# Moving the rows of the 64x64 inverses from GpSimd to VectorE in a DeltaNet decoder step, with their blocks packed in DRAM

## The chip, the cores and the metric

The kernel runs on one core of a Trainium2 chip. The core has a matrix engine (PE in the profile) with its weight load (PEld), VectorE (DVE), ScalarE (ACT), GpSimd (POOL) and SyncE (SP), on whose queue all DMAs of this kernel are issued. Each engine runs its own instructions strictly in the order of the program and waits for the others by semaphores. The metric is the device time of one execution in microseconds; the program is timed several times and the median is given. One execution was also taken by the hardware profiler, and all rows shown here come from it.

## What is computed

A prompt of 1040 tokens (16 learned ones and 1024 given ones) and 64 sample tokens go through two decoder layers. The change touches the first mixer, a gated DeltaNet with 8 heads, in which every chunk of 64 tokens of a head needs the inverse of a unit lower triangular 64x64 matrix:

```python
kk = jnp.einsum('bhnid,bhnjd->bhnij', k, k)
lower = jnp.where(strict, beta[..., :, None] * kk * decay, 0.0)
T = lax.linalg.triangular_solve(lower + eye, jnp.broadcast_to(eye, lower.shape),
                                left_side=True, lower=True, unit_diagonal=True)
U = jnp.einsum('bhnij,bhnje->bhnie', T, v * beta[..., None])
W = jnp.einsum('bhnij,bhnjd->bhnid', T, k * (beta * jnp.exp(G))[..., None])
```

Before it stand the projections of q, k, v and z (the gate), a short causal convolution and SiLU on q, k and v, SiLU alone on z, and a normalisation of k. Everything else (the recurrence, the output projection, two ConvFFNs and a pooling mixer) is the same in both kernels.

## The kernel before

The projection stage makes 33 tiles of 128 output channels in the order of the list `order`: a tile with the decay inputs (`ba`), then k, v and z tiles of the first heads, k3 to k7, q0 to q7, and then v and z in turn from v2, z2 to v7, z7. A tile is three chunks of 368 tokens, c0 to c2. For a chunk PE runs 24 matmuls into one of four PSUM banks (`a_chunk`, `a_half`, `mm3`: three products of high and low halves for each of 8 blocks of input channels). For q, k and v the chunk is convolved: one scaling on ACT and three multiply-adds on DVE (L384), in c2 three more for the sample tokens (L389), then SiLU on ACT (L257). A z chunk goes from PSUM through SiLU on ACT and needs nothing of DVE. A bank is free again when ACT and DVE have read it. The weights come in tiles of 128x512, which ACT and POOL split in two halves (L154, L155, `wlo`), two for each tile. A finished tile is written to DRAM (`spill`, L512).

For every k tile a job (`k_steps`) follows that lies between the chunks of the next tiles: it loads the decay row `Gb` and the beta row `Bb` by a broadcast (L483, L484), makes the decay matrices `E` on DVE (L489), normalises k, multiplies k by itself on PE, multiplies the products by `E` into `Q` (L503), sets the diagonal on POOL (L504) and writes the 128x1152 tile `Q` to DRAM as `Qd` (L508).

After the last head the inverses begin (`inverses`, `invert`). 128 blocks of 64x64 (8 heads, 16 chunks) lie one to a partition in `Qb`, read from `Qd` by 16 DMAs (L541), and a set of 40 blocks of 16x16 for the last tokens lies in `Qt`, read by 5 DMAs (L545). For every column j an outer product (L529) and a subtraction (L531) are run on the columns behind it. Rows 0 to 9 of the inverse are on POOL (`Xa`, `ta`), rows 10 to 63 on DVE (`Xb`, `tb`), and the 16x16 blocks (`Xt`) use `tb` too. `tb` is also the source of a DMA that fills a DRAM tile with zeros (L553). The results are written to DRAM (`xb`), turned block by block (3 copies on DVE, one on POOL, L565 and L568), and written again (`xt`).

The inverses are a generator that the projection loop advances: after every chunk it gets `INV` more of a budget, and each step takes the cost that it yields. So the place of the inverse's instructions in DVE's and POOL's order is set when the program is built, by these numbers, and not by what has arrived. When it is done, the loads of head 0 and the first Newton step (`after_inverses`, `newton`) are put between the chunks that are left, and the recurrence over heads begins after the last tile, z7.

Of the kernel before, what the change touches and what calls it, by code (L numbers as in the profile page):

```python
# [10 lines left out]
F32 = mybir.dt.float32  # L11
F32R = mybir.dt.float32r
AF = mybir.ActivationFunctionType
ALU = mybir.AluOpType
# [3 lines left out]
P = 128  # L18
# [14 lines left out]
H = 8  # L33
# [5 lines left out]
GROUPS = ((0, 3), (3, 3), (6, 3))  # L39
NEWTON = ((0, 3), (3, 3), (6, 2))  # L40
GW = 384
PROWS = 10
TAIL0 = 1024
INV = 2.4
NTAIL = N_META + NSA


# [150 lines left out]
def build(nc, tc, I, O, stop=None):  # L198
    es = ExitStack()
    V, A, G, T, SY = nc.vector, nc.scalar, nc.gpsimd, nc.tensor, nc.sync  # L200
    slots = Slots()

    def pool(name, bufs=1, ctx=es, space=None, side=None):
        kw = {"reuse_waits": "tile", "side": side}
        if space == DRAM:
            kw = {"space": space}
        elif space == PSUM:
            kw = {"space": space, "reuse_waits": "tile"}
        return ctx.enter_context(tc.tile_pool(name=name, bufs=bufs, **kw))
# [124 lines left out]
    zd_d = [dr.tile([P, NTP], F32, name=f"zd{h}") for h in range(H)]  # L334
    Qd_d = dr.tile([H, P, NTP], F32, name="Qd")

    xb_d = dr.tile([P, 4096], F32, name="xb")
    xt_d = dr.tile([P, 4096], F32, name="xt")
    x8_d = dr.tile([H, NTAIL, NTAIL], F32, name="x8")
# [12 lines left out]

    AHEAD = 4
    order = [("ba", 0), ("k", 0), ("k", 1), ("k", 2), ("v", 0), ("z", 0), ("v", 1), ("z", 1)]
    order += [("k", h) for h in range(3, H)] + [("q", h) for h in range(H)]
    for h in range(2, H):
        order += [("v", h), ("z", h)]
    base = {"q": 0, "k": 8, "v": 16, "z": 24}
    tid = [32 if kd == "ba" else base[kd] + h for kd, h in order]

# [41 lines left out]
    def l2norm(dst):  # L402

        while busy:
            yield 1
        busy.append(dst)
        sq = ab.tile([P, NT], F32, tag="sq", name="sq")
        rr = ab.tile([P, NT], F32, tag="rr", name="rr")
        A.activation(sq, dst[:, :NT], AF.Square)
        yield 3  # L410
        hl = []
        for c in range(NCH):
            hl.append([kp.tile([P, CH], F32R, tag=nm, name=nm, bufs=3) for nm in ("sqh", "sql")])
# [12 lines left out]
        busy.pop()
# [51 lines left out]
    def k_steps(h, kT):  # L478
        while busy or not rows[0].done or h > 1 and not kj[h - 2].done:
            yield 1  # L480
        Gb = kp.tile([P, NTP], F32, tag="Gb", name="Gb")
        Bb = kp.tile([P, NTP], F32, tag="Bb", name="Bb")
        SY.dma_start(out=Gb, in_=grow_d[h:h + 1, :].partition_broadcast(P))  # L483
        SY.dma_start(out=Bb, in_=brow_d[h:h + 1, :].partition_broadcast(P))  # L484
        E = kp.tile([P, NTP], F32, tag="E", name="E", bufs=2)
        for u in range(NU):
            s = slice(u * P, (u + 1) * P)
            m = cm[:, K_MF:K_MF + P] if u < 8 else cm[:, K_MT:K_MT + P]
            V.scalar_tensor_tensor(E[:, s], Gb[:, s], cols[:, u, 1, h:h + 1], m,  # L489
                                   op0=ALU.subtract, op1=ALU.add)  # L490
        yield from l2norm(kT)
        A.activation(E, E, AF.Exp)
        G.tensor_tensor(E, E, Bb, op=ALU.mult)
        Q = kp.tile([P, NU, P], F32, tag="Q", name="Q", bufs=2)
        yield 7
        SY.dma_start(out=kd_d[h], in_=kT)
        for g0, gn in GROUPS:
            ps = px.tile([P, 3, P], F32, tag="px", name="kk")
            for u in range(gn):
                s = slice((g0 + u) * P, (g0 + u + 1) * P)  # L500
                T.matmul(ps[:, u, :], kT[:, s], kT[:, s], start=True, stop=True)
            q = Q[:, g0:g0 + gn, :]
            V.tensor_tensor(q, ps, v3(E[:, g0 * P:(g0 + gn) * P]), op=ALU.mult)  # L503
            G.affine_select(q, q, pattern=[[0, gn], [1, P]], compare_op=ALU.not_equal, fill=1.0,  # L504
                            base=0, channel_multiplier=-1)
            yield 1
        yield 1
        SY.dma_start(out=Qd_d[h], in_=flat(Q))  # L508

    def spill(dd, t):  # L510
        yield 2
        SY.dma_start(out=dd, in_=t)  # L512

    def invert(parts, Qb, n, m):


        for eng, r0, X, tmp in parts:
            G.memset(X[:n], 0.0)
            G.memset(X[:n].rearrange("p a b -> p (a b)")[:, r0::m + 1], 1.0)
        yield 1.0  # L520
        for j in range(m - 1):
            w = m - 1 - j
            cost = 0.0
            for eng, r0, X, tmp in parts:
                k = min(j + 1 - r0, X.shape[1])
                if k <= 0:
                    continue
                t = tmp[:n, 0:k * w].rearrange("p (a b) -> p a b", b=w)
                eng.tensor_tensor(t, X[:n, 0:k, j:j + 1].to_broadcast([n, k, w]),  # L529
                                  Qb[:n, j:j + 1, j + 1:m].to_broadcast([n, k, w]), op=ALU.mult)  # L530
                eng.tensor_tensor(X[:n, 0:k, j + 1:m], X[:n, 0:k, j + 1:m], t, op=ALU.subtract)  # L531
                cost = max(cost, 0.25 + k * w * (0.0033 if eng is G else 0.0021))
            yield cost

    def inverses(sp):
        Qb = sp.tile([P, 64, 64], F32, name="Qb")
        Qt = sp.tile([P, 16, 16], F32, name="Qt")
        for h in range(H):
            for a in range(2):
                src = Qd_d[h][64 * a:64 * a + 64, :].rearrange("j (u t) -> u j t", t=P)  # L540
                SY.dma_start(out=Qb[64 * a + 8 * h:64 * a + 8 * h + 8], in_=src[0:8, :, 64 * a:64 * a + 64])  # L541
        nt = NTAIL // 16
        for a in range(nt):
            r = slice(16 * a, 16 * a + 16)
            SY.dma_start(out=Qt[8 * a:8 * a + 8], in_=Qd_d[:, r, TAIL0 + 16 * a:TAIL0 + 16 * a + 16])  # L545
        Xa = sp.tile([P, PROWS, 64], F32, name="Xa")
        Xb = sp.tile([P, 64 - PROWS, 64], F32, name="Xb")
        ta = sp.tile([P, PROWS * (64 - PROWS)], F32, name="ta")
        tb = sp.tile([P, 1024], F32, name="tb")
        t8 = tb[:NTAIL, :H * NTAIL]  # L550
        Xt = sp.tile([P, 16, 16], F32, name="Xt")
        G.memset(t8, 0.0)
        SY.dma_start(out=x8_d.rearrange("h p t -> p h t"), in_=v3(t8, NTAIL))  # L553
        yield 6.0
        tail = invert([(V, 0, Xt, tb)], Qt, 8 * nt, 16)
        for cost in invert([(G, 0, Xa, ta), (V, PROWS, Xb, tb)], Qb, P, 64):
            next(tail, None)
            yield cost
        for a in range(nt):
            r = slice(16 * a, 16 * a + 16)  # L560
            SY.dma_start(out=x8_d[:, r, 16 * a:16 * a + 16], in_=Xt[8 * a:8 * a + 8])
        XT = Qb.rearrange("p b a -> p a b")
        SY.dma_start(out=xb_d[:, 0:64 * PROWS], in_=flat(Xa))
        SY.dma_start(out=xb_d[:, 64 * PROWS:], in_=flat(Xb))
        G.tensor_copy(XT[:, 0:PROWS, :], Xa)  # L565
        for r in range(0, 64 - PROWS, 18):
            n = min(r + 18, 64 - PROWS)
            V.tensor_copy(XT[:, PROWS + r:PROWS + n, :], Xb[:, r:n, :])  # L568
            yield 1.0
        SY.dma_start(out=xt_d, in_=flat(Qb))  # L570
        yield 1.0
# [72 lines left out]
    with ExitStack() as en:  # L644
# [16 lines left out]
        for nm in ("sq", "rr"):  # L661
            t = ab.tile([P, NT], F32, tag=nm, name=nm)
# [450 lines left out]
    r0 = []  # L1113
# [418 lines left out]
    for pos, (l, i, hf, c) in enumerate(units):  # L1532
# [23 lines left out]
        n = 0  # L1556
# [138 lines left out]
```

## Time and profile before

| | us |
|---|---|
| median of 3 runs | 2599.67 |
| lowest and highest | 2596.69 and 2604.51 |
| time of the profiled execution | 2598.88 |
| span of its trace | 2597.1 |
| PE busy | 2410.2 (93%) |
| DVE busy | 1647.3 (63%) |
| POOL busy | 1167.5 (45%) |
| ACT busy | 1022.4 (39%) |

The profiled execution's own time is 1.8 us more than its span; the span is what the trace covers. The share of an engine is over the whole span and mixes stages with different limits. The stage of this change ends 541 us after the start of the span.

### The profile page before, as it was taken

The page shows a single profiled execution, that of the slowest core. Times are in us where ns is not written, and L with a number is a line of the kernel's source. Part 1 is how long each engine was busy: PE and PEld are TensorE (multiplying, and loading weights), DVE is VectorE, ACT ScalarE, POOL GpSimd, SP SyncE. Part 2 cuts the span into 40 slices and gives each one's busy share as a digit, 9 for nine tenths or more (in the row PEclk, how much of TensorE's full clock was granted, in tenths as well). Part 3 has the DMA queues.
Part 4 walks back from the last instruction along what each step waited for, and adds up shares of the span by engine and source line. Part 5 has one row for each costly group of instructions (what it writes and reads, how often), then busy time and mean ns, then how long its engine had stood idle before and what let it go on. Part 6 is the DMA issues. An engine that isn't in the chain of part 4 may idle for free.

```text
span 2597.1 us, 38494 instructions
## 1 busy us (share of the span) xinstructions
PE 2410.2 (93%) x14341; PEld 2350.7 (91%) x14341; DVE 1647.3 (63%) x3139; ACT 1022.4 (39%) x2165; POOL 1167.5 (45%) x1232
## 2 busy tenths in 40 slices
PE   6899588978999889999999999888999999999997
PEld 5898587978888789999999999877899999999996
DVE  7678399856666655555555546887964555555556
ACT  5667122255454543222222344445354323222234
POOL 3456388644554443233322455466465333233342
PEclk9999799999999999999999999999999999999999
DMA  3254612467552211111111133233433111111112
GB/s 132 96 178 170 97 70 78 143 215 237 173 167 67 75 57 50 41 49 41 49 41 41 62 106 106 82 104 110 91 102 107 50 49 41 41 49 45 46 53 81
DMA packets 139802, 233.31 MB, mean 90 GB/s; under 512 B 48848, under 2 KB 59472, under 8 KB 139360
## 3 DMA queue, kind: packets, MB, share of 16 engines
q1 hardware_dynamic: 139616, 230.86, 27.4%
q8 instruction: 113, 1.85, 0.3%
q14 instruction: 73, 0.60, 0.1%
HBM read 191.77 MB, written 39.04 MB: 89 GB/s over the span
## 4 chain that ended last, share of the span: by engine, by line
PE 67%; DVE 18%; issue 4%; ACT 4%; POOL 3%; DMA 2%; SPq 2%; DVEq 0%; POOLq 0%; ACTq 0%
PE up L265 12%; PE up L263 12%; PE up L264 12%; PE dn L265 6%; PE dn L263 6%; PE dn L264 6%; DVE acc L384 2%; POOL wlo L155 2%; DVE tb L529 2%; PE ps L263 2%; DVE Xb L531 2%; PE ps L264 2%; PE ps L265 2%; DVE nhf L318 1%; SPq L541 1%
## 5 line engine op out<-in xcount | busy, mean ns | idle before, releaser
L155 POOL TENSOR_TENSOR wlo<-wst,whi 128x512 fp32r<-128x512 f32 x470 | 629.2, 1357 | 515.1 <-ACT whi L154 503.9
L263 PE MATMUL up<-hhi,whi 128*128 128x370 f32 (+2 forms) x2112 | 708.9, 336 | 0.7 <-ACT hhi L321 0.7
L264 PE MATMUL up<-hlo,whi 128*128 128x370 f32 (+2 forms) x2112 | 699.8, 331 | 2.7 <-DVE hlo L324 1.8
L265 PE MATMUL up<-hhi,wlo 128*128 128x370 f32 (+2 forms) x2112 | 701.6, 332 | 0.0
L1272 DVE SCALAR_TENSOR_TENSOR acc<-up,cv,acc 128x368 f32<-128x368 f32 (+4 forms) x528 | 303.7, 575 | 625.1 <-ACT acc L1264 387.6
L1336 DVE TENSOR_TENSOR xT<-xT,dn 128x368 f32<-128x368 f32 (+1 forms) x864 | 409.0, 527 | 2.3 <-PE dn L265 2.3
L264 PEld LDWEIGHTS up<-hlo,whi 128*128 128x128 f32 x2112 | 401.8, 190 | 5.9 <-DVE hlo L324 2.2
L263 PEld LDWEIGHTS up<-hhi,whi 128*128 128x128 f32 x2112 | 400.5, 190 | 3.0 <-ACT hhi L321 1.0
L265 PEld LDWEIGHTS up<-hhi,wlo 128*128 128x128 f32 x2112 | 399.9, 189 | 0.0
L263 PE MATMUL dn<-ghi,whi 128*128 128x368 f32 (+1 forms) x1056 | 352.8, 334 | 21.6 <-ACT acc L257 8.8
L1310 POOL TENSOR_TENSOR glo<-acc,ghi 128x368 fp32r<-128x368 f32 (+1 forms) x132 | 133.2, 1009 | 484.1 <-ACT ghi L1309 477.9
L265 PE MATMUL dn<-ghi,wlo 128*128 128x368 f32 (+1 forms) x1056 | 349.2, 331 | 0.5 <-POOL wlo L155 0.5
L264 PE MATMUL dn<-glo,whi 128*128 128x368 f32 (+1 forms) x1056 | 348.9, 330 | 0.3 <-POOL glo L1310 0.3
L1264 ACT ACTIVATE acc<-up,cv 128x368 f32<-128x368 f32 (+1 forms) x264 | 173.1, 656 | 429.7 <-PE up L265 427.8
L263 PE MATMUL ps<-hhi,whi 128*128 128x368 f32 (+1 forms) x792 | 273.1, 345 | 58.7 <-DVE tb L529 28.5
L154 ACT CAST whi<-wst 128x512 fp32r<-128x512 f32 x470 | 275.0, 617 | 75.4 <-PE up L264 50.1
L264 PE MATMUL ps<-hlo,whi 128*128 128x368 f32 (+1 forms) x792 | 269.5, 340 | 5.2 <-DVE hlo L324 3.8
L265 PE MATMUL ps<-hhi,wlo 128*128 128x368 f32 (+1 forms) x792 | 267.7, 338 | 0.0
L263 PEld LDWEIGHTS dn<-ghi,whi 128*128 128x128 f32 x1056 | 200.6, 190 | 25.8 <-DVE xT L1336 7.8
L263 PEld LDWEIGHTS ps<-hhi,whi 128*128 128x128 f32 x792 | 154.0, 194 | 66.1 <-issue 59.0
L264 PEld LDWEIGHTS dn<-glo,whi 128*128 128x128 f32 x1056 | 200.6, 190 | 2.0 <-POOL glo L1310 0.6
L265 PEld LDWEIGHTS dn<-ghi,wlo 128*128 128x128 f32 x1056 | 200.5, 190 | 1.0 <-POOL wlo L155 1.0
(212 smaller groups left out, 3375.6 us busy)
## 6 DMA issues: line engine op xcount, KB each, us to landing
wst<-i_w_up SPq DMA_DIRECT2D x272, 256.0 KB
wst<-i_w_dn SPq DMA_DIRECT2D x120, 256.0 KB
wst<-i_w_in SPq DMA_DIRECT2D x62, 256.0 KB
Gb<-grow SPq DMA_DIRECT2D x8, 576.0 KB
Bb<-brow SPq DMA_DIRECT2D x8, 576.0 KB
vd<-out SPq DMA_DIRECT2D x8, 576.0 KB
zd<-out SPq DMA_DIRECT2D x8, 576.0 KB
kd<-out SPq DMA_DIRECT2D x8, 576.0 KB
```

The lines of the kernel that those rows point to most:

```text
L154: self.nc.scalar.copy(hi, st)
L155: self.nc.gpsimd.tensor_tensor(lo, st, hi.bitcast(F32), op=ALU.subtract)
L263: T.matmul(ps, hi[:, ws], rhi(k), start=start and j == 0, stop=False)
L264: T.matmul(ps, hi[:, ws], rlo(k), start=False, stop=False)
L265: T.matmul(ps, lo[:, ws], rhi(k), start=False, stop=stop and j == n - 1)
L384: V.scalar_tensor_tensor(acc[:, a:n], ps[:, o + a - d:o + n - d], w[3 - d], acc[:, a:n], op0=ALU.mult, op1=ALU.add)
L529: eng.tensor_tensor(t, X[:n, 0:k, j:j + 1].to_broadcast([n, k, w]), Qb[:n, j:j + 1, j + 1:m].to_broadcast([n, k, w]), op=ALU.mult)
L531: eng.tensor_tensor(X[:n, 0:k, j + 1:m], X[:n, 0:k, j + 1:m], t, op=ALU.subtract)
L1264: A.activation(acc[:, b:], ps[:, o + b:o + CH], AF.Identity, scale=w[2], bias=col(C_FCB + l * NUP + n))
L1272: V.scalar_tensor_tensor(acc[:, i:m], ps[:, o + i - d:o + m - d], w[2 - d], acc[:, i:m], op0=ALU.mult, op1=ALU.add)
L1310: G.tensor_tensor(glo, acc, ghi.bitcast(F32), op=ALU.subtract)
L1336: V.tensor_tensor(xT[:, m, s], xT[:, m, s], ps[:, b:CH], op=ALU.add)
```

## The change

Five things change.

1. `k_steps` writes, beside the whole `Q` (`Qd`), its sixteen 64x64 diagonal blocks to a new DRAM tile `qb`, by two DMAs per head ahead of the one for `Qd`; `inverses` reads all 128 blocks of `Qb` from there by one DMA.
2. All 64 rows of the inverse are in one tile `X` and run on DVE, 63 pairs of instructions of up to 32x32 elements per partition; POOL has no part in it but the two memsets, which now stand ahead of the first step. The cost that a step yields is 0.13 + 0.0021 for each element, and `INV` is 2.8.
3. The 16x16 blocks have a scratch tile of their own (`tt`), are read after the first steps (`yield 8.0`), and are begun in the ninth step.
4. The turning copies are four copies of 16 rows on ACT.
5. The z tiles are spread: after k7 the order is q0 q1 z2, q2 q3 z3, q4 q5 z4, q6 q7 z5, v2 v3 v4 z6, v5 v6 v7 z7.

```diff
-INV = 2.4
+INV = 2.8
+    qb_d = dr.tile([P, 64, 64], F32, name="qb")
-    order += [("k", h) for h in range(3, H)] + [("q", h) for h in range(H)]
-    for h in range(2, H):
-        order += [("v", h), ("z", h)]
+    order += [("k", h) for h in range(3, H)]
+    for x in ("q0 q1 z2", "q2 q3 z3", "q4 q5 z4", "q6 q7 z5", "v2 v3 v4 z6", "v5 v6 v7 z7"):
+        order += [(t[0], int(t[1])) for t in x.split()]
...
+        for a in range(2):
+            b = slice(64 * a, 64 * a + 64)
+            SY.dma_start(out=qb_d[64 * a + 8 * h:64 * a + 8 * h + 8].rearrange("u j t -> j u t"), in_=Q[b, 0:8, b])
         SY.dma_start(out=Qd_d[h], in_=flat(Q))
...
+    def invert(X, tmp, Qb, n, m):
         for j in range(m - 1):
-            w = m - 1 - j
...
+            w, k = m - 1 - j, j + 1
+            t = tmp[:n, 0:k * w].rearrange("p (a b) -> p a b", b=w)
+            V.tensor_tensor(t, X[:n, 0:k, j:j + 1].to_broadcast([n, k, w]),
+                            Qb[:n, j:j + 1, j + 1:m].to_broadcast([n, k, w]), op=ALU.mult)
+            V.tensor_tensor(X[:n, 0:k, j + 1:m], X[:n, 0:k, j + 1:m], t, op=ALU.subtract)
+            yield 0.13 + k * w * 0.0021
...
-        for h in range(H):
-            for a in range(2):
-                src = Qd_d[h][64 * a:64 * a + 64, :].rearrange("j (u t) -> u j t", t=P)
-                SY.dma_start(out=Qb[64 * a + 8 * h:64 * a + 8 * h + 8], in_=src[0:8, :, 64 * a:64 * a + 64])
...
+        SY.dma_start(out=Qb, in_=qb_d)
+        X = sp.tile([P, 64, 64], F32, name="X")
...
+        yield 8.0
...
+        tt = sp.tile([P, 64], F32, name="tt")
+        tail = invert(Xt, tt, Qt, 8 * nt, 16)
+        for j, cost in enumerate(invert(X, tb, Qb, P, 64)):
+            if j >= 8:
+                cost += 2 * next(tail, 0.0)
             yield cost
...
-        SY.dma_start(out=xb_d[:, 0:64 * PROWS], in_=flat(Xa))
-        SY.dma_start(out=xb_d[:, 64 * PROWS:], in_=flat(Xb))
-        G.tensor_copy(XT[:, 0:PROWS, :], Xa)
-        for r in range(0, 64 - PROWS, 18):
-            n = min(r + 18, 64 - PROWS)
-            V.tensor_copy(XT[:, PROWS + r:PROWS + n, :], Xb[:, r:n, :])
+        SY.dma_start(out=xb_d, in_=flat(X))
+        for r in range(0, 64, 16):
+            A.copy(XT[:, r:r + 16, :], X[:, r:r + 16, :])
             yield 1.0
```

How the change moves instructions is seen on two engines. First the SP queue, where the DMAs are issued, around a head's `Q` in the phase of the k tiles (`Qd` is the whole `Q` in DRAM, `qb` its packed blocks, `Gb` and `Bb` the rows that the next head's `E` needs, `wst` a weight tile). Before:

```order
59 L162 DMA wst<-i_w_in 128x512
60 L508 DMA Qd<-Q 128x1152
61 L483 DMA Gb<-grow 128x1152
62 L484 DMA Bb<-brow 128x1152
63 L162 DMA wst<-i_w_in 128x512
```

After:

```order
64 L161 DMA wst<-i_w_in 128x512
65 L511 DMA qb<-Q 64x8x64 x2
66 L512 DMA Qd<-Q 128x1152
67 L484 DMA Gb<-grow 128x1152
68 L485 DMA Bb<-brow 128x1152
```

The two writes of blocks stand ahead of `Qd` and so ahead of the next head's `Gb` and `Bb`. At the end of the k phase the same queue held, before, the 16 reads of `Qb`, the five of `Qt` and the zeros (`x<-tb`) ahead of the next spill and weights:

```order
71 L508 DMA Qd<-Q 128x1152
72 L541 DMA Qb<-Qd 8x64x64 x16
73 L545 DMA Qt<-Qd 8x16x16 x5
74 L553 DMA x_109<-tb 80x8x80
75 L512 DMA qd_83<-out 128x1152
76 L162 DMA wst<-i_w_in 128x512 x2
```

After:

```order
79 L512 DMA Qd<-Q 128x1152
80 L531 DMA Qb<-qb 128x4096
81 L537 DMA x_110<-tb 80x8x80
82 L516 DMA qd_83<-out 128x1152
83 L161 DMA wst<-i_w_in 128x512 x2
84 L545 DMA Qt<-Qd 8x16x16 x5
```

One read takes the place of sixteen, and the small ones go behind the weights. Then DVE's order from the last product `Q` of head 7 on (`acc<-ps` are the convolutions of a chunk, `tb` and `X` the steps of the inverse). Before:

```order
152 L503 TENSOR_TENSOR Q<-kk,E 128x384
153 L384 SCALAR_TENSOR_TENSOR acc<-ps,cv,acc 128x367
154 L384 SCALAR_TENSOR_TENSOR acc<-ps,cv,acc 128x366
155 L384 SCALAR_TENSOR_TENSOR acc<-ps,cv,acc 128x365
156 L384 SCALAR_TENSOR_TENSOR acc<-ps,cv,acc 128x368 x3
157 L384 SCALAR_TENSOR_TENSOR acc<-ps,cv,acc 128x304 x3
158 L389 SCALAR_TENSOR_TENSOR acc<-raw,cv,acc 128x64 x3
159 L529 TENSOR_TENSOR tb<-Xt,Qt 40x15
```

After:

```order
152 L504 TENSOR_TENSOR Q<-kk,E 128x384
153 L523 TENSOR_TENSOR tb<-X,Qb 128x63
154 L525 TENSOR_TENSOR X<-X,tb 128x63
155 L523 TENSOR_TENSOR tb<-X,Qb 128x124
156 L525 TENSOR_TENSOR X<-X,tb 128x2x62
157 L385 SCALAR_TENSOR_TENSOR acc<-ps,cv,acc 128x367
```

The convolutions of a whole tile (q2) that stood ahead of the first step are gone from there, because a z tile now lies at this place. Last, ACT's order at the end of the inverses in the new kernel (the copies `Qb<-X` turn the blocks, `out` are the SiLUs, `whi` the split of weights):

```order
329 L256 ACTIVATE out<-ps 128x368
330 L558 COPY Qb<-X 128x16x64
331 L153 CAST whi<-wst 128x512 x2
332 L256 ACTIVATE out<-ps 128x368
333 L558 COPY Qb<-X 128x16x64 x2
334 L377 ACTIVATE acc<-ps,cv 128x368
```

The first copy stands ahead of the weights' split and of the SiLU of a z chunk.

## Rows read from the trace of the kernel before

**Rows 1.** Stretches: busy us (instructions) of PE, PEld, DVE, ACT, POOL; clock; DMA share, GB/s.
```profile
264.60:289.00 24.40, 24.40 (x145) 24.13 (x143) 5.97 (x12) 5.76 (x13) 7.58 (x11) 1.00 0.63 69
289.00:315.40 26.40, 0.04 (x1) 0.00 (x0) 2.31 (x6) 0.00 (x0) 3.14 (x8) 0.58 0.76 94
315.40:505.00 189.60, 168.08 (x937) 164.23 (x938) 183.35 (x243) 46.65 (x112) 157.22 (x178) 0.96 0.22 79
505.00:541.00 36.00, 36.00 (x227) 36.00 (x227) 13.77 (x29) 8.30 (x23) 3.37 (x8) 1.00 0.70 253
```
**Rows 2.** Waits from 265 to 532 us: us in total, times, longest us.
```profile
DVE tb L529 <- DMA x<-tb: 36.5, 1, 36.5
```
**Rows 3.** Timeline of SP: start us, us, engine line op out<-in xcount.
```profile
264.63 0.32 SPq L508 DMA_DIRECT2D Qd<-Q  x1
267.48 35.77 SPq L541 DMA_DIRECT2D Qb<-Qd  x16
```
**Rows 4.** Timeline of PE, in brackets the idle time before and its releaser.
```profile
100.80 0.65 PE L263 MATMUL ps<-hhi,whi 128*128 128x368 f32 x1 [5.07 <-DVE acc L384]
...
315.43 0.65 PE L263 MATMUL ps<-hhi,whi 128*128 128x372 f32 x1 [26.39 <-DVE tb L529]
...
529.09 0.83 PE L774 MATMUL nw<-Tbd,lQ 128*128 128x128 f32 x6
```
**Rows 5.** Chain of waits in the k phase, 228 to 262 us: start us, us, what.
```profile
237.12 4.80 DMA Gb<-grow
241.94 5.13 DVE E L489 x9
...
249.46 1.04 PE ss L422 x4
```
**Rows 6.** Timeline of DVE: a decay matrix, convolutions, steps of the inverse.
```profile
146.41 6.82 DVE L489 SCALAR_TENSOR_TENSOR E<-Gb,cols,cm 128x128 f32<-128x128 f32 x9 [1.19 <-DMA Gb<-grow]
...
332.21 0.22 DVE L531 TENSOR_TENSOR Xt<-Xt,tb 40x63 f32<-40x63 f32 x1
...
381.13 1.86 DVE L384 SCALAR_TENSOR_TENSOR acc<-ps,cv,acc 128x368 f32<-128x368 f32 x3
...
385.34 1.66 DVE L384 SCALAR_TENSOR_TENSOR acc<-ps,cv,acc 128x304 f32<-128x304 f32 x3
...
436.52 0.90 DVE L529 TENSOR_TENSOR tb<-Xb,Qb 128x728 f32<-128x728 f32 x1
...
446.08 1.23 DVE L531 TENSOR_TENSOR Xb<-Xb,tb 128x725 f32<-128x725 f32 x1
...
468.94 1.79 DVE L529 TENSOR_TENSOR tb<-Xb,Qb 128x629 f32<-128x629 f32 x1
...
497.08 0.42 DVE L529 TENSOR_TENSOR tb<-Xb,Qb 128x245 f32<-128x245 f32 x1
...
527.62 0.92 DVE L389 SCALAR_TENSOR_TENSOR acc<-raw,cv,acc 128x64 f32<-128x64 f32 x3
```
**Rows 7.** Timeline of POOL beside them.
```profile
446.62 1.13 POOL L529 TENSOR_TENSOR ta<-Xa,Qb 128x220 f32<-128x220 f32 x1
...
468.18 3.71 POOL L155 TENSOR_TENSOR wlo<-wst,whi 128x512 fp32r<-128x512 f32 x2
...
513.07 0.95 POOL L798 MEMSET Xbd<- 128x1024 f32 x1 [6.36 <-DMA xt<-Qb]
```
**Rows 8.** Issues of Tbd loads, ns min/median/max; two stretches with small pieces, columns as Rows 1.
```profile
L739 SPq DMA_DIRECT2D Tbd<-xt x16: 574/626/1524, 515.0 to 779.6; - x16
...
309.00:311.00 2.00, 0.00 (x0) 0.00 (x0) 0.00 (x0) 0.00 (x0) 0.00 (x0) 0.50 1.09 93
781.00:784.50 3.50, 3.50 (x27) 3.27 (x27) 3.23 (x12) 1.16 (x3) 1.04 (x2) 1.00 1.20 167
```
**Rows 9.** Groups of the page: the split of a weight tile; busy us, mean ns, idle before.
```profile
L155 POOL TENSOR_TENSOR wlo<-wst,whi 128x512 fp32r<-128x512 f32 x470 | 629.2, 1357 | 515.1 <-ACT whi L154 503.9
...
L154 ACT CAST whi<-wst 128x512 fp32r<-128x512 f32 x470 | 275.0, 617 | 75.4 <-PE up L264 50.1
```

More of the change, by code (lines that the diff above doesn't have):

```diff
@@ L41 @@
 GW = 384
-PROWS = 10
 TAIL0 = 1024
-INV = 2.4
+INV = 2.8
 NTAIL = N_META + NSA
@@ L512, in spill @@
         SY.dma_start(out=dd, in_=t)
[L514 to L520, printed above, removed]
-        for j in range(m - 1):
-            w = m - 1 - j
[L523 to L533, printed above, removed]
+    def invert(X, tmp, Qb, n, m):
+        for j in range(m - 1):
+            w, k = m - 1 - j, j + 1
[4 more added lines that the diff above has]
+            yield 0.13 + k * w * 0.0021
     def inverses(sp):
@@ L537, in inverses @@
         Qt = sp.tile([P, 16, 16], F32, name="Qt")
-        for h in range(H):
-            for a in range(2):
-                src = Qd_d[h][64 * a:64 * a + 64, :].rearrange("j (u t) -> u j t", t=P)
-                SY.dma_start(out=Qb[64 * a + 8 * h:64 * a + 8 * h + 8], in_=src[0:8, :, 64 * a:64 * a + 64])
[L542 to L548, printed above, removed]
+        SY.dma_start(out=Qb, in_=qb_d)
+        X = sp.tile([P, 64, 64], F32, name="X")
         tb = sp.tile([P, 1024], F32, name="tb")
@@ L553, in inverses @@
         SY.dma_start(out=x8_d.rearrange("h p t -> p h t"), in_=v3(t8, NTAIL))
[L554 to L557, printed above, removed]
+        for x, m in ((X, 64), (Xt, 16)):
+            G.memset(x, 0.0)
+            G.memset(flat(x)[:, ::m + 1], 1.0)
+        yield 8.0
+        nt = NTAIL // 16
+        for a in range(nt):
+            r = slice(16 * a, 16 * a + 16)
+            SY.dma_start(out=Qt[8 * a:8 * a + 8], in_=Qd_d[:, r, TAIL0 + 16 * a:TAIL0 + 16 * a + 16])
+        tt = sp.tile([P, 64], F32, name="tt")
[3 more added lines that the diff above has]
+                cost += 2 * next(tail, 0.0)
             yield cost
```

## The prediction

> **What bounds the kernel now.** I read the stretches first, then the waits, then the queue behind the longest wait, and last the chain of waits in the phase before. I count from T0, 264.6 us, when head 7's `Q` is complete; the projections end at 541.0, so this stage takes 24.4 + 26.4 + 189.6 + 36.0 = 276.4 us [rows 1]. Three things are to be seen in it. First, PE stands still for 26.39 us, and what released it was DVE's first step of the inverse [rows 4]: DVE had itself waited 36.5 us for a DMA, the zeros written out of `tb` [rows 2], which stood on SP's queue behind sixteen reads of `Qb` that took 35.77 us to issue [rows 3]. The convolutions behind that step on DVE could not run, the four PSUM banks stayed full, PE stopped. Its clock fell to the lower level (the mean is 0.58 in that stretch, 1.00 before it, [rows 1]). Second, from 315.4 to 505 DVE is busy 183.35 of 189.6 us and PE only 168.08: here DVE is the bound, PE loses 21.5 us in short waits. Third, POOL is busy 157 us in this stretch and makes DVE slow: a step of 629 columns takes 1.79 us beside a weight's split `wlo` on POOL [rows 6, 7]. By the steps of 245 and 728 columns (0.42 and 0.90 us, [rows 6]) a column costs 0.99 ns and an instruction 0.18, so alone it would take 0.80.
>
> What PE needs alone is a floor: 24.40 us hold 145 matmuls [rows 1], 0.168 each, a chunk of 24 takes 4.04, the 18 tiles after T0 have 54 chunks: 218 us, and head 0's Newton products add some 3 (six records in at most 0.83, [rows 4], 32 records). The stage could end at T0 + 221.
>
> **The change part by part, after T0.** *The wait for the blocks.* The DVE order shows that the first step now stands right behind the last `Q`, with the z tile z2 in front of PE: 3 chunks, 12.1 us, that DVE has no part in, and four banks behind it. Ahead of the step lie head 7's two block writes (2.8 us, below) and their landing (2.85 us from `Qd`'s issue to the read that waited for it, [rows 3]), so the one read is issued near T0 + 5.5. It moves 2 MB, and a store of 2 MB kept POOL waiting 6.36 us [rows 7]; the zeros behind it are 0.2 MB at 93 GB/s [rows 8], 2.2 us. DVE starts near T0 + 15. PE would stop for this at T0 + 12.1 + 4 x 4.04 = T0 + 28 only, so the 26.39 us go, and the low clock with them. What is late next is DVE.
>
> *DVE's sum.* Column j takes two instructions of (j + 1)(63 - j) elements; over 63 columns that is 2 x 43,680 elements and 126 instructions: 86.5 + 22.7 us, and 0.03 between two of them, 4: 113 us. The 16x16 blocks: 30 instructions at 0.22 [rows 6] and the gaps, 7. Ahead of the last step DVE's order has the convolutions of nine tiles (q2 to q7, v2 to v4), each 2 x 1.86 + 1.66 + 0.92 = 6.3 [rows 6]: 57. POOL now has only its weights: 12 tiles with two splits, each of which cost a step 1.0 us more; steps are two thirds of DVE's time, so 16 of the 24 meet one: 16 us. I take this from 5 (most meet convolutions) to 33 (all 24 cost a split's mean length, 1.357 [rows 9]). Sum: 113 + 7 + 57 + 16 = 193. So DVE gets 35 us more work of its own (34,890 elements that POOL had) and loses the slowing by the 126 POOL instructions of the inverse. It is the bound all the same: the last step ends near T0 + 15 + 193 = T0 + 208.
>
> *Behind the last step.* On ACT the first turning copy waits for it, and behind the copy wait two weight splits and a z chunk's SiLU, which frees a bank. PE is by then four banks ahead, at v6 c0, and goes on 3 us later: a copy of 1,024 columns at twice the 0.617 of a split with 512 [rows 9], two splits and a SiLU. The other copies hold the next convolution's scaling, which I price at 1.5 more. Nine chunks are left, 36.4, and Newton, 3: T0 + 208 + 3 + 1.5 + 36.4 + 3 = T0 + 252. The turned blocks and head 0's loads have 30 us of chunks to hide under; before, they had 27 from the step at 501 to the Newton products at 529.09 [rows 4], and PE did not wait. The z tiles and the copies taken from DVE cost nothing of their own. So the stage takes 252 instead of 276.4: **-24.4 us**.
>
> **The change ahead of T0.** This part costs. Of the k phase the chain of waits shows a closed loop: `Q` is done, SP issues `Qd` and then the next head's `Gb`, `Gb` lands 4.80 us later, DVE makes `E` from it, and then come the convolution, a SiLU and PE's `ss` [rows 5]. DVE waits for `Gb` at five heads (the first 1.19 us, at 146.41 [rows 6], the last at 241.94), and at the last three PE waits at the end of this chain. The SP order puts two block writes ahead of `Qd` and `Gb`; whatever they take is added. Each moves 128 KB in pieces of 256 B. The trace has no such write. The nearest rows: the `Tbd` loads, the same shape the other way, of which four and little else moved at 167 GB/s, 0.8 us each; the zeros, a write in pieces of 320 B, at 93 GB/s, 1.4 us each [rows 8]; and the sixteen old `Qb` reads, 35.77 / 16 = 2.2 us each by their issue [rows 3]. The least is the issue alone, 2 x 0.6 = 1.2 us [rows 8]. So a pair costs 1.2 to 4.5 us; I take 2.6, near the zeros, since that is a write too. At three heads: **+7.8 us** (3.6 at the least; 22 if all five heads pass on 4.5). `Bb` and the next weights are queued behind the writes too; no wait for them is in that chain, so I price their delay at nothing.
>
> Sum, against the profiled execution's 2598.88 (span 2597.1 and 1.8 around it; the median of the three runs, 2599.67, is 0.8 more): 2598.9 - 24.4 + 7.8 = 2582.3, rounded 2582.
>
> **The Trainium skill against these rows.** Row 446.08 of DVE and 446.62 of POOL [rows 6, 7] overlap, a step of 725 columns taking 1.23 instead of 0.90: both went on, slower. "SBUF — State Buffer", section "SBUF: two separate sides", says instead that a VectorE instruction with two SBUF inputs and a GpSimd one that reads SBUF hold a shared port pair in turn, each for its whole length. By that rule every split that meets a step costs all of it; that is rival 2. "DMA: Bandwidth & Descriptors", section "Specifications", says that transfers under 512 B go by read-modify-write, which speaks against the block writes; the rows agree in kind, 93 GB/s for the zeros [rows 8] against 253 on average where mostly whole rows move [rows 1]. That is rival 1, if the price is high.
>
> **The rivals.** *1. The block writes hold the k phase.* For it: the loop has no slack, five waits for `Gb`. Against it: at the first two PE is never idle, and nearest loads are fast. With 4.5 us at all five heads, +22: 2598.9 - 24.4 + 22 = 2597, no change. It is slower than before from 32 us on, 6.5 per head: writes of 2.6 us each and the 1.2 of issue make 6.4, and a gap like that brings the low clock (after the gap of 5.07 us a matmul took 0.65 us, [rows 4]), some 2 us at three heads. Then 2598.9 - 24.4 + 32 + 6 = 2612. *2. POOL blocks DVE fully*, 33 instead of 16: the stage takes 269 and the sum is 2599. For it the row of 1.79 us, in which a whole us is lost; against it, that a convolution beside POOL shows none. *3. Both prices are at their low ends* (5 instead of 16 us, 1.2 instead of 2.6 per head): 2582.3 - 11 - 4.2 = 2567. *4. It doesn't do what it says*: the one read comes so late that DVE holds PE again. A landing after T0 + 28 is needed; the 2 MB would have to take 20 us instead of 6.4. Then every us of the start is a us of the end, and with 15 us later it is 2597.
>
> **How the numbers follow.** Chances: forecast (2575 to 2591) 0.55; rival 3, 0.19; rival 1 at no change 0.08 and slower 0.06; rival 2, 0.09; rival 4, 0.03. This kernel's measurement can tell about 0.3%, 7.8 us, from no change: faster is below 2592. Faster is 0.55 + 0.19 = 0.74, the same 0.08 + 0.09 + 0.03 = 0.20, slower 0.06. For 8 in 10 the range reaches to rival 3's time on the one side and past the three rivals at 2597 to 2599 on the other: 2566 to 2602; what is left out is slower than that, or a DVE without any loss.
>
> **What would show it.** The stretch from head 7's last `Q` to the last projection takes near 252 us instead of 276.4, with no PE wait over some 6 us in it and a clock near 1.00. DVE's first step starts 13 to 17 us after that `Q`, the 126 steps are 113 us and 10 to 25 more by POOL, and DVE is busy almost without a gap until the last of them. The last `Q` itself comes 4 to 12 us later than 264.6, by later landings of `Gb`, 7.4 us behind the first block write instead of 4.8 behind `Gb`'s own issue. I am wrong if `Gb` lands over 10 us after `Q`, if a PE wait of 10 us or more stands behind the turning copies on ACT, or if the Newton products wait for their loads.

## The result, and the profile after

The median of four runs is 2583.43 us (2583.05 to 2585.50) against 2600.79 (2596.69 to 2604.51) for the kernel before in the same comparison: a ratio of 0.9935, 95% interval 0.9918 to 0.9952, so about 17 us faster. The forecast was 2582. The profiled execution took 2583.61 us with a span of 2581.5.

Three stretches of the changed kernel answer to [rows 1]: from head 7's `Q` (T0, 270.0 us now) to the first step of the inverse, from there to the end of the last step, and from there to the first product of the recurrence (`pc`). The columns are those of [rows 1].

```profile
270.00:284.60 14.60, 14.60 (x89) 14.60 (x88) 0.00 (x0) 3.55 (x7) 7.23 (x8) 1.00 0.81 254
284.60:474.80 190.20, 170.37 (x968) 167.04 (x967) 183.91 (x264) 44.38 (x106) 48.53 (x54) 0.97 0.21 75
474.80:525.00 50.20, 43.97 (x264) 43.14 (x262) 21.41 (x46) 24.43 (x49) 7.47 (x16) 0.97 0.65 234
```

While DVE waits for its blocks (0.00 busy), PE is busy the whole 14.6 us: the stretch with 0.04 us of PE and the clock at 0.58 [rows 1] is gone. In the second stretch DVE is busy 183.9 of 190.2 us and PE 170.4: DVE is the bound, as before. SP's queue and DVE's first step, which answer to [rows 2, 3]:

```profile
270.00 1.27 SPq L511 DMA_DIRECT2D qb<-Q  x2
271.32 0.63 SPq L512 DMA_DIRECT2D Qd<-Q  x1
275.14 0.33 SPq L531 DMA_DIRECT2D Qb<-qb  x1
275.56 0.49 SPq L537 DMA_DIRECT2D x<-tb  x1
```

```profile
284.65 0.22 DVE L523 TENSOR_TENSOR tb<-X,Qb 128x63 f32<-128x63 f32 x1 [15.28 <-DMA x<-tb]
...
474.56 0.28 DVE L525 TENSOR_TENSOR X<-X,tb 128x63 f32<-128x63 f32 x1
482.21 1.24 DVE L385 SCALAR_TENSOR_TENSOR acc<-ps,cv,acc 128x367 f32<-128x367 f32 x2 [7.37 <-ACT acc L377]
```

The one read goes out 5.1 us after T0, the first step runs at T0 + 14.6 instead of T0 + 48.3, the last ends at T0 + 204.8. Behind it DVE stands still for 7.37 us: ACT is at the turning copies and scales no convolution. The lines with `COPY` are the first copy, and the next two together:

```profile
474.87 1.93 ACT L558 COPY Qb<-X 128x1024 f32<-128x1024 f32 x1 [9.44 <-DVE X L525]
...
478.02 3.80 ACT L558 COPY Qb<-X 128x1024 f32<-128x1024 f32 x2
481.60 0.57 ACT L377 ACTIVATE acc<-ps,cv 128x368 f32<-128x368 f32 x1
```

In the k phase the chain of waits now reads as follows (start, length, what), against [rows 5]:

```profile
242.93 7.02 DMA Gb<-grow
249.97 2.45 DVE E L490 x9
...
254.82 1.04 PE ss L423 x4
```

`Gb` lands 7.02 us after its issue instead of 4.80, since the block writes move beside it (with the writes behind it, in the run late_writes below, DVE waits 1.90 us for it and not 6.18). But the nine operations of `E` take 2.45 us instead of 5.13. Last, the recurrence, which the change does not touch, gave some of the gain back. Here are 11.5 us of it from about the same instruction on, the changed kernel first and then the one before:

```profile
578.90:590.40 11.50, 10.06 (x44) 8.80 (x45) 5.18 (x13) 8.04 (x25) 4.84 (x5) 0.58 0.80 212
```

```profile
598.50:610.00 11.50, 9.93 (x64) 8.65 (x65) 5.58 (x15) 9.80 (x31) 5.59 (x6) 0.85 0.98 259
```

At a granted clock of 0.58 PE gets through 44 matmuls where it made 64 at 0.85. The first product `pc` came 20.5 us earlier than before (525.0 against 545.5), the end only 15.6.

### The profile page after: what moved, and what is told of

It reads as the page before. It is cut to its first block, busy times and chain, and to the rows that moved or that the text cites. A ratio compares the mean times of both kernels' runs of the same rounds, so it can differ in the third digit from the quotient of the medians.

```text
span 2581.5 us, 38414 instructions
## 1 busy us (share of the span) xinstructions
PE 2415.2 (94%) x14341; PEld 2355.8 (91%) x14341; DVE 1629.9 (63%) x3156; ACT 1029.1 (40%) x2169; POOL 1056.6 (41%) x1103
## 4 chain that ended last, share of the span: by engine, by line
PE 67%; DVE 20%; ACT 5%; issue 3%; POOL 3%; DMA 2%; SPq 0%; DVEq 0%; POOLq 0%; ACTq 0%
PE up L262 12%; PE up L264 12%; PE up L263 12%; PE dn L264 6%; PE dn L262 6%; PE dn L263 6%; DVE acc L385 3%; DVE tb L523 2%; DVE X L525 2%; POOL wlo L154 2%; DVE nhf L317 1%; PE ps L262 1%; PE ps L263 1%; PE ps L264 1%; DVE acc L1262 1%
```

## The experiments

All kernels are read by the same marks. T0 is when head 7's `Q` is complete, read from the first DMA on SP that writes it out. "From ss" is the time to T0 from the first gap of PE at `ss` (at 140 to 143 us in every trace), which takes out what differs before the k phase. "Rest" is the span behind `pc`. The ratio is to the kernel before in the same comparison.

| kernel | median us | ratio (95%) | from ss | first step | last step ends | last step to pc | T0 to pc | rest |
|---|---|---|---|---|---|---|---|---|
| before | 2600.8 | 1 | 124.7 | T0+48.3 | T0+236.9 | 44.0 | 280.9 | 2051.6 |
| changed | 2583.4 | 0.9935 (0.9918-0.9952) | 128.3 | 14.6 | 204.8 | 50.2 | 255.0 | 2056.5 |
| u_reads | 2608.4 | 1.0028 (1.0010-1.0046) | 123.1 | 48.7 | 238.9 | 50.4 | 289.3 | 2054.2 |
| u_rows | 2579.6 | 0.9921 (0.9891-0.9951) | 128.7 | 15.0 | 209.0 | 45.5 | 254.5 | 2053.8 |
| u_order | 2585.9 | 0.9943 (0.9925-0.9962) | 131.7 | 14.5 | 205.2 | 50.1 | 255.3 | 2057.0 |
| p_reads | 2576.8 | 0.9914 (0.9881-0.9948) | 131.1 | 15.3 | 204.2 | 44.0 | 248.2 | 2061.5 |
| late_writes | 2578.2 | 0.9912 (0.9895-0.9928) | 123.5 | 14.7 | 204.9 | 50.4 | 255.4 | 2054.4 |
| gb_early | 2574.4 | 0.9895 (0.9876-0.9913) | 117.0 | 14.6 | 204.7 | 50.4 | 255.2 | 2058.4 |
| copies_dve | 2582.3 | 0.9920 (0.9900-0.9939) | 129.0 | 15.2 | 207.3 | 45.6 | 252.9 | 2051.5 |
| z_early | 2580.7 | 0.9923 (0.9905-0.9941) | 131.4 | 14.5 | 198.8 | 53.8 | 252.6 | 2058.1 |
| tt_psum | 2584.7 (one run) | | 130.6 | 14.9 | 201.9 | 50.4 | 252.3 | 2058.1 |
| best1 | 2567.6 | 0.9865 (0.9848-0.9882) | 117.0 | 15.0 | 201.3 | 50.7 | 252.0 | 2053.9 |
| best1_pace | 2563.5 | 0.9851 (0.9834-0.9869) | 117.0 | 15.0 | 204.4 | 43.8 | 248.2 | 2053.9 |
| best3 | 2561.1 | 0.9838 (0.9820-0.9856) | 118.5 | 15.0 | 204.3 | 44.0 | 248.3 | 2050.0 |

**Which part carries the gain.** Four kernels take the change apart. The first keeps all but the packed blocks (u_reads):

```diff
-            SY.dma_start(out=qb_d[64 * a + 8 * h:64 * a + 8 * h + 8].rearrange("u j t -> j u t"), in_=Q[b, 0:8, b])
...
-        SY.dma_start(out=Qb, in_=qb_d)
+        for h in range(H):
+            for a in range(2):
+                src = Qd_d[h][64 * a:64 * a + 64, :].rearrange("j (u t) -> u j t", t=P)
+                SY.dma_start(out=Qb[64 * a + 8 * h:64 * a + 8 * h + 8], in_=src[0:8, :, 64 * a:64 * a + 64])
```

> The changed kernel with the sixteen old reads of Qb out of Qd, and without the block writes per head. Theory A (the one read is what carries the gain): the reads take 35.8 us to issue again, the zeros and with them DVE's first step come near T0 + 41 instead of T0 + 14.7; PE, which has z2 and four banks in front of it, stops from about T0 + 28, 13 to 15 us long, and its clock falls; DVE, the bound, ends some 18 us later, of which the k phase gives back 3 to 5 without the writes: near 2598 us, as before the change. Rival B (the reads were hidden anyway, the rows on DVE and the order of the tiles carry the gain): no PE stall over 6 us and 2583 less the writes' 3 to 5: 2579.

It took 2608.4 us. The queue holds DVE again, and PE stands behind it (SP's queue, then PE):

```profile
267.01 36.12 SPq L530 DMA_DIRECT2D Qb<-Qd  x16
303.24 2.54 SPq L536 DMA_DIRECT2D x<-tb  x1
```

```profile
288.15 0.33 PE L264 MATMUL ps<-hhi,wlo 128*128 128x368 f32 x1
315.96 0.65 PE L262 MATMUL ps<-hhi,whi 128*128 128x372 f32 x1 [27.47 <-DVE acc L384]
```

Theory A named the right mechanism, but its numbers were too small (it expected 2598): the first step came at T0 + 48.7 and not at 41, 9.7 us behind the issue of the zeros at 303.24, and PE stopped at T0 + 24, not 28. So without the one read the rest of the change costs 0.1 to 0.5%, with T0 to `pc` 8.4 us longer than before.

The second has the packed blocks and the new order, with the inverses as before: rows 0 to 9 on POOL, copies on DVE and POOL, pace 2.4 (u_rows):

```diff
-INV = 2.8
+INV = 2.4
...
-        tail = invert(Xt, tt, Qt, 8 * nt, 16)
-        for j, cost in enumerate(invert(X, tb, Qb, P, 64)):
+        tail = invert([(V, 0, Xt, tb)], Qt, 8 * nt, 16)
+        for cost in invert([(G, 0, Xa, ta), (V, PROWS, Xb, tb)], Qb, P, 64):
```

> The changed kernel with the inverses as before (rows 0 to 9 on POOL, pace 2.4, turning copies on DVE and POOL, 16x16 blocks from the start), but with the block writes, the one read and the new order of tiles. Theory A (a POOL instruction with two inputs in SBUF takes about 1 us from a DVE step that meets it, whatever the step's length, so POOL's 126 instructions cost DVE more than the 35 us of work that they spare it): 5 to 20 us slower than the changed kernel, 2588 to 2603. Rival B (POOL's rows come for little; the read and the order are the whole gain): DVE's sum falls by about 30 us, PE becomes the bound of the stage, 2570 to 2580.

It took 2579.6 us, which can't be told from the changed kernel (their intervals overlap); T0 to `pc` is 254.5 against 255.0. Theory A fell. The time is rival B's, but not its reason: DVE is still busy 187.7 of the 194.0 us between first and last step.

The third has the old order of the tiles (u_order):

```diff
-    for x in ("q0 q1 z2", "q2 q3 z3", "q4 q5 z4", "q6 q7 z5", "v2 v3 v4 z6", "v5 v6 v7 z7"):
-        order += [(t[0], int(t[1])) for t in x.split()]
+    order += [("q", h) for h in range(H)]
+    for h in range(2, H):
+        order += [("v", h), ("z", h)]
```

> The changed kernel with the old order of the tiles (all q, then v and z in turn). Theory A (DVE is the bound, so each tile without a convolution that stands ahead of the last step is a tile's 12 us for PE at no cost to DVE): about one tile's convolutions more ahead of the last step (6.3 us) and a first wait of PE, since the four banks are full at T0 + 16 and the first step is at T0 + 15: 2588 to 2595. Rival B (the order does nothing, since PE is not the bound there): 2583 within 3 us.

2585.9 us, T0 to `pc` 255.3: no difference, rival B.

The fourth is the kernel before with the block writes and the one read, nothing else (p_reads):

> The kernel before with the block writes and the one read alone; POOL's rows, the copies and the order of the tiles stay as they were. Theory A of the prediction (the 26.4 us stall of PE is the term that pays): the stall goes, DVE starts some 26 to 36 us earlier, the k phase loses 3 to 5: 2575 to 2582, no slower than the changed kernel. Rival B (with POOL's rows in the way and the q tiles all ahead, DVE stays the bound and most of the stall comes back in short waits): 2588 to 2596.

2576.8 us, theory A; its interval overlaps that of the changed kernel, so it is no slower, and not shown to be faster. The stretches T0 to first step, first to last step, last step to `pc`:

```profile
272.60:287.90 15.30, 15.30 (x92) 15.30 (x91) 5.96 (x12) 5.19 (x12) 8.11 (x15) 1.00 0.76 243
287.90:476.80 188.90, 169.82 (x971) 165.90 (x970) 182.63 (x244) 47.10 (x111) 159.72 (x185) 0.98 0.22 77
476.80:520.90 44.10, 40.79 (x259) 40.55 (x257) 18.71 (x37) 13.23 (x35) 5.14 (x10) 0.99 0.73 258
```

With POOL busy 160 us DVE and PE do the same in p_reads as with POOL busy 48 in the changed kernel: 971 matmuls in 188.9 us against 968 in 190.2. So the packed blocks are the gain. The rows on DVE, their pace, the copies on ACT and the order of the tiles add nothing that can be measured in the medians, and from T0 to `pc` they cost 6.8 us in the traces, 6.2 of them behind the last step (50.2 instead of 44.0).

**Why the rows gain nothing.** I compared each of DVE's steps with its length alone (0.18 us and 0.99 ns a column, from [rows 6]). Before, the 136 steps take 121.0 us where alone they would take 77.8: 43.2 go to POOL's instructions. Changed, the 156 steps take 136.6 instead of 115.9. So 38 us of work came to DVE's steps and 22.5 us of waiting left them. The convolutions lost some of their waiting too. Between the first and the last step both kernels run the same ones: 81 multiply-adds on a chunk, which read PSUM, and 27 on the sample tokens, which read `raw` and `acc` in SBUF. Each line has the shortest, median and longest in ns, the kernel before first:

```profile
L384 DVE SCALAR_TENSOR_TENSOR acc<-ps,cv,acc x81: 518/589/604, 313.4 to 487.9; 128x368 f32<-128x368 f32 x27, 128x304 f32<-128x304 f32 x27, 128x367 f32<-128x367 f32 x9, 128x366 f32<-128x366 f32 x9
L389 DVE SCALAR_TENSOR_TENSOR acc<-raw,cv,acc x27: 277/672/1344, 324.1 to 489.1; 128x64 f32<-128x64 f32 x27
```

```profile
L385 DVE SCALAR_TENSOR_TENSOR acc<-ps,cv,acc x81: 519/594/602, 285.7 to 463.1; 128x368 f32<-128x368 f32 x27, 128x304 f32<-128x304 f32 x27, 128x367 f32<-128x367 f32 x9, 128x366 f32<-128x366 f32 x9
L390 DVE SCALAR_TENSOR_TENSOR acc<-raw,cv,acc x27: 274/285/286, 300.6 to 464.2; 128x64 f32<-128x64 f32 x27
```

The 81 take 46.5 us in both; the 27 take 19.8 us before (and in p_reads) and 7.6 in the changed kernel. So 38 us of work were moved for 22.5 + 12.2 = 34.7 us of waiting, which accounts for the stretch having about the same length (188.5 us before, 188.9 in p_reads, 190.2 changed). The last step ends at T0 + 204 or 205 in p_reads and in the changed kernel.

What a meeting costs is to be seen at a weight's two splits on POOL in the changed kernel (DVE first, then POOL):

```profile
335.44 1.07 DVE L525 TENSOR_TENSOR X<-X,tb 128x880 f32<-128x880 f32 x1
336.43 1.29 DVE L523 TENSOR_TENSOR tt<-Xt,Qt 40x48 f32<-40x48 f32 x1
337.76 1.21 DVE L525 TENSOR_TENSOR Xt<-Xt,tt 40x48 f32<-40x48 f32 x1
...
335.69 3.22 POOL L154 TENSOR_TENSOR wlo<-wst,whi 128x512 fp32r<-128x512 f32 x2 [12.35 <-ACT whi L153]
```

The step of 880 columns, which began first, took its normal 1.07; the two of 48 columns took 1.29 and 1.21 where 0.23 is normal. Of 156 steps 21 lost over 0.25 us, and each of the 21 began while a split was running: 18 with 1.09 to 1.24 us of it left lost 0.96 to 1.07, whether they had 15 or 1,023 columns, and 3 with 0.68 to 0.71 left lost 0.56 to 0.60. So a step loses what is left of the split, less 0.1 to 0.2 us. One of the 3 (DVE, then POOL; the second split ends at 399.33):

```profile
398.62 1.78 DVE L523 TENSOR_TENSOR tb<-X,Qb 128x1015 f32<-128x1015 f32 x1
```

```profile
395.81 3.52 POOL L154 TENSOR_TENSOR wlo<-wst,whi 128x512 fp32r<-128x512 f32 x2 [11.75 <-ACT whi L153]
399.28 1.19 POOL L380 COPY raw<-cst 128x24 f32<-128x24 f32 x1
```

The small copy `raw`, 0.21 us where nothing holds it, ends with DVE's step: there POOL waits for DVE. A rate that both share would have cost the long steps more. They take turns. One run asks what it depends on (tt_psum):

```diff
-        tt = sp.tile([P, 64], F32, name="tt")
+        tt = px.tile([P, 512], F32, tag="px", name="tt")[:, 0:64]
```

> The changed kernel with the scratch of the 16x16 steps, tt, in PSUM. In the changed kernel four pairs of these steps meet a weight's split on POOL, and both steps of a pair take 1.2 to 1.3 us instead of 0.23. Theory A (while an instruction with two inputs in SBUF runs on POOL, a DVE instruction with two inputs in SBUF stands still, whatever its length, and one with an input in PSUM doesn't): the product tt<-Xt,Qt still takes near 1.3 us when it meets a split, the difference Xt<-Xt,tt, whose second input is now in PSUM, takes 0.2 to 0.3 beside one. Rival B (POOL slows all of DVE's traffic to SBUF): both still take 1.2 to 1.3 us. The time as a whole within 4 us of 2583.

```profile
337.80 1.30 DVE L523 TENSOR_TENSOR tt<-Xt,Qt 40x48 f32<-40x48 f32 x1
339.13 0.20 DVE L525 TENSOR_TENSOR Xt<-Xt,tt 40x48 f32<-40x48 f32 x1
```

```profile
337.06 3.21 POOL L154 TENSOR_TENSOR wlo<-wst,whi 128x512 fp32r<-128x512 f32 x2 [12.24 <-ACT whi L153]
```

The product, with two inputs in SBUF, takes 1.30 again; the difference, with one input in PSUM, takes 0.20 in the middle of the second split. All four pairs read alike (0.20, 0.21, 0.20 and 0.18). Theory A holds, and it fits the convolutions: those that read PSUM showed no loss, those that read only SBUF did. "SBUF — State Buffer" of the Trainium skill, section "SBUF: two separate sides", states this: a DVE instruction with two SBUF inputs and a GpSimd one that reads SBUF exclude each other for their whole length, and the one that starts first goes first. The trace agrees: a step waits until the split is nearly done, 1.0 us where 1.1 to 1.2 of the split were left.

**The k phase.** The block writes behind the next head's loads (late_writes; `blocks` holds a head's two writes), and the next head's `Gb` loaded as soon as its buffer is free (gb_early):

```diff
         SY.dma_start(out=Bb, in_=brow_d[h:h + 1, :].partition_broadcast(P))
+        while bw:
+            bw.pop(0)()
...
+        bw.append(blocks)
```

```diff
-        Gb = kp.tile([P, NTP], F32, tag="Gb", name="Gb")
+        Gb = gbs.pop(h) if h in gbs else gb_load(h)
...
-        yield from l2norm(kT)
+        for n, cost in enumerate(l2norm(kT)):
+            if n == 1 and h + 1 < H:
+                gbs[h + 1] = gb_load(h + 1)
+            yield cost
```

> The changed kernel with a head's two block writes behind the next head's Gb and Bb on SP's queue instead of ahead of Qd. Theory A (the prediction's term: the writes delay Gb by 3.9 us a head, and that is on the path at three heads): Gb lands 4.8 us behind its issue again, DVE waits 1 to 3 us for it instead of 3.8 to 7.0, head 7's Q is complete 6 to 8 us earlier, 2576 us. Rival B (what the writes cost comes back because E, made later, no longer runs beside POOL's splits: its nine operations took 2.45 us instead of 5.13): E takes about 5 us again, head 7's Q is within 3 us of where it was, 2581 to 2584.

> The changed kernel with the next head's Gb loaded as soon as its buffer is free, some 15 us before E needs it. Theory A (PE's gaps at ss in the k phase, 0.8 + 3.6 + 1.2 + 2.8 us, hang on the landing of Gb): DVE doesn't wait for Gb any more, the gaps go, head 7's Q comes 6 to 8 us earlier: 2575 to 2578. Rival B (something else closes that loop, E beside POOL at 5 us or the weights that now stand behind Gb on SP's queue): gaps of the same size in other places, 2581 to 2586.

In late_writes DVE waits less, and `E` is slow again, 5.56 us. It starts while POOL makes the splits of `sq`; in the changed kernel it starts at 249.97, when POOL's last instruction there has just ended (248.67 + 1.30). DVE and POOL of late_writes, then POOL of the changed kernel:

```profile
243.51 5.56 DVE L494 SCALAR_TENSOR_TENSOR E<-Gb,cols,cm 128x128 f32<-128x128 f32 x9 [1.90 <-DMA Gb<-grow]
...
244.62 1.96 POOL L416 TENSOR_TENSOR sql<-sq,sqh 128x368 fp32r<-128x368 f32 x2 [0.27 <-ACT sqh L415]
246.53 1.34 POOL L154 TENSOR_TENSOR wlo<-wst,whi 128x512 fp32r<-128x512 f32 x1
```

```profile
246.81 1.91 POOL L416 TENSOR_TENSOR sql<-sq,sqh 128x368 fp32r<-128x368 f32 x2 [0.28 <-ACT sqh L415]
248.67 1.30 POOL L154 TENSOR_TENSOR wlo<-wst,whi 128x512 fp32r<-128x512 f32 x1
```

T0 comes 3.3 us earlier, 4.8 from `ss`, and the median is 2578.2: theory B in `E`, in T0 between the two, nearer B, and in the median between them, nearer A's 2576. In gb_early DVE doesn't wait for `Gb` from the second head on. The 99 us to 259, gb_early first, then the changed kernel:

```profile
160.00:259.00 99.00, 99.00 (x624) 99.00 (x623) 75.74 (x150) 73.44 (x126) 60.62 (x74) 1.00 0.61 200
```

```profile
160.00:259.00 99.00, 90.58 (x551) 88.82 (x550) 62.37 (x135) 67.06 (x114) 54.06 (x65) 0.98 0.54 171
```

PE never stops there; T0 is at 259.2, 10.8 us earlier, and the median is 2574.4 us, 9 less: theory A, and more than the 6 to 8 us that it expected. The last five `E` took 3.2 to 4.3 us there, and PE did not wait for them.

**Behind the last step.** The copies on DVE (copies_dve: `A.copy` to `V.tensor_copy`), and the z tiles still earlier (z_early; the added `flush(0)` runs the SiLUs that are still pending, since a v tile now comes last):

```diff
-    for x in ("q0 q1 z2", "q2 q3 z3", "q4 q5 z4", "q6 q7 z5", "v2 v3 v4 z6", "v5 v6 v7 z7"):
+    for x in ("q0 q1 z2", "q2 z3 q3", "q4 z4 q5", "q6 z5 q7", "v2 z6 v3 z7", "v4 v5 v6 v7"):
...
+    flush(0)
```

> The changed kernel with the four turning copies on DVE instead of ACT. Theory A (ACT's copies, 2.0 us each, hold the convolutions' scaling; DVE stands idle for 7.4 us behind its last step): DVE makes the copies itself in 4 x 1.1 us, ACT is free, the stage ends about 3 us earlier: 2580. Rival B (PE has four banks ahead, so the copies' place shows nothing): 2583.

> The changed kernel with the z tiles still earlier: a z after each q or v, and only v4 to v7 behind the last step. Theory A (from DVE's start to its last step PE loses 22 us in short waits because DVE is the bound; a z tile gives PE 12 us of work that DVE has no part in, and one tile's convolutions, 6.3 us, move behind the last step): the last step ends 6 us earlier, 2577. Rival B (the order gave nothing so far: the kernel with the old order took 2586 against 2583, and the same may hold again): 2583 within 3 us.

DVE of copies_dve behind the last step:

```profile
476.58 2.94 DVE L558 COPY Qb<-X 128x1024 f32<-128x1024 f32 x3
479.36 1.84 DVE L385 SCALAR_TENSOR_TENSOR acc<-ps,cv,acc 128x367 f32<-128x367 f32 x3
481.12 1.08 DVE L558 COPY Qb<-X 128x1024 f32<-128x1024 f32 x1
```

A copy takes DVE 1.0 to 1.1 us, ACT 1.9 to 2.1. The last step to `pc` falls from 50.2 to 45.6 us, but the last step ends 2.5 us later: 2.1 us net in the trace, nothing that the medians can tell (2582.3; theory A expected 2580). In z_early the last step ends 6.0 us earlier, as theory A expected, and 3.6 of them are lost behind it: 2.4 us net, 2580.7 instead of A's 2577, not to be told from no change.

**All together.** best1 is gb_early, copies_dve and z_early at once; best1_pace has `INV` 2.7 besides; best3 is p_reads with gb_early's edit.

> The changed kernel with three edits at once: the next head's Gb loaded early, the z tiles still earlier, the turning copies on DVE. Theory A (the k phase and the stage behind it are worth their sum): 2574 for the first, 2.5 us less by each of the others, as their traces show from head 7's Q to the first product of the recurrence: 2569. Rival B (only the k phase counts, the rest drowns in the recurrence's clock): 2574.

> As the kernel with the three edits, with the pace of the inverses at 2.7 instead of 2.8, by which the last step and the Newton products stand two chunks later. Theory A (PE has 6 us less to do behind the last step, and DVE, the bound, gets two chunks' convolutions more ahead of it): 2 to 4 us less than with 2.8: 2566. Rival B (the loads of the turned blocks are no longer hidden): the Newton products wait, 2570 to 2576.

> The kernel before with the block writes, the one read and the early Gb alone: POOL keeps its rows, the order of the tiles and the copies stay as before the change. Theory A (the rows on DVE and the new order of the tiles add nothing; from head 7's Q to the first product of the recurrence the kernel with the two reads alone took 248.2 us, the changed one 255.0): 2564 to 2570, faster than the changed kernel with the early Gb, 2574. Rival B (the rows on DVE and the order pay once the k phase no longer holds): 2574 or more.

best1 took 2567.6 us, near theory A's 2569, though its interval still touches that of gb_early. With a pace of 2.7 T0 to `pc` falls by 3.8 us, as expected, to 248.2; the median falls by 4.1, with intervals that overlap. best3 took 2561.1 us, theory A and 3 us below its range, and is the fastest: 1.6% below the kernel before. Its interval lies below that of gb_early, which has the same k phase. Of its 13 us to gb_early 6.9 are between T0 and `pc`; 8.4 are in the recurrence of the profiled executions, which no edit touches, and T0 itself is 2.2 later.

## Why the prediction was right, and where it was not

The mechanism was right: the wait for the blocks went, and the k phase gave some of it back. That the total came within 1.2 us of the median is luck, for its errors cancelled. From the profiled executions: T0 comes 5.4 us later instead of 7.8, T0 to `pc` is 25.9 us shorter instead of 24.4, and 4.9 us are lost behind `pc` that no step had: 2582.3 - 2.4 - 1.5 + 4.9 = 2583.3.

- **The wait for the blocks** was right: first step at T0 + 14.6 (forecast 15), no PE stall over 4.3 us between T0 and `pc`. It is the whole gain: p_reads has it alone, u_reads all but it. The prediction didn't price the other parts on their own. It could have: its 35 us of moved work stood beside "loses the slowing by the 126 POOL instructions" without a number for that, and the trace before shows what POOL costs: 43.2 us in the steps and some 12 in the multiply-adds on the sample tokens.
- **DVE's sum** was right as a sum: 190.2 us between first and last step (193), 136.6 of it steps (113 + 7 + 16 = 136), with 20.7 for POOL instead of 16. The nine tiles of convolutions took 54.2 instead of 57.
- **The reading of rows 446.08 and 446.62** failed. "Both went on, slower", the prediction said [rows 6, 7], since the two spans overlap. But a span holds the wait for the other engine. The mechanism of rival 2 is what happens; its 33 us were too many because it charged each split's whole 1.357 us and let all 24 meet a step. 21 met one, 18 at 1.0 and 3 at 0.6, since the step began when part of the split was over.
- **Behind the last step**: 44 us forecast to the last projection, 45.4 measured. The copies cost about what was priced (3 + 1.5; taking them off ACT gives 4.6), although one takes 2.0 us and not 1.2: PE had banks ahead, and its longest wait there was 2.73 us.
- **Ahead of T0** the size was nearly right and the working was not. A pair of block writes delays `Gb` by 3.8 us (9.1 from `Q` to `E` instead of 5.3) and not 2.6. But `E` then no longer meets POOL and gives 2.7 back, which no step had. From `ss` to T0 the seven profiles that have the writes in this place and `Gb` in its old one take 128.3 to 131.7 us, the two without writes 123.1 and 124.7, the one with late writes 123.5: 4 to 9 us, at the low end of the bounds of 3.6 to 22.
- **What was left out**: the recurrence. Behind `pc` the same code took 2050.0 to 2061.5 us in the 14 profiles above, with a mean granted clock of 0.76 to 0.90 in its first 50 us. Ten us of this can hide or feign a gain; it isn't a property of the edits as far as the runs show. The four executions of p_reads alone lie between 2572.9 and 2584.2 us, and its profile, with the 2061.5, is of the slowest of them. Whether when a kernel enters the recurrence decides its clock stays open.

## What to carry to other kernels

When a bound engine's first instruction waits for loads, pack what it needs as it is produced and bring it in one transfer; here that was the whole gain, and the redistribution of work beside it was worth nothing. Before work is moved from GpSimd to VectorE, compare each VectorE instruction's time, the convolutions' too, with its time alone: what is lost to turns is the most that can come back, and it has to be set against the work that moves. A load that stands in a closed loop is first taken out of the loop, by an earlier issue into a buffer that is free, before anything is placed ahead of it.

## What was not expected of the hardware

- A DVE step with two SBUF inputs that begins during a 128x512 split on POOL loses what is left of the split, less 0.1 to 0.2 us, whatever its own length (0.96 to 1.07 us with 15 to 1,023 columns, 0.56 to 0.60 where 0.7 was left); with one input in PSUM it loses nothing (0.18 to 0.21 us beside the same split).
- A later landing made `E` faster: 2.45 us behind POOL's splits, 5.13 and 5.56 beside them.
- ACT turns a block of 128x1024 in 1.9 to 2.1 us, DVE in 1.0 to 1.1.
- Two writes of 128 KB in pieces of 256 B take SP 1.27 us to issue, and the load behind them lands 2.2 us later after its own issue (7.02 instead of 4.80).
